# Start bytes of the moving operands: inner activations to byte 192, inputs of the second block and of the last feed-forward to byte 128

## The chip, the core and the metric

The kernel runs on one core of one Trainium2 chip. The metric is the device time of one execution in microseconds; the time before is the median of three runs. The profile is of one further execution, whose own time is given beside its span.

## What is computed

One sequence of 256 tokens with 1024 features, and 256 context tokens, go through two residual blocks of two layers each. All data are float32.

```
first_block, per layer:  h = half_ffn(h); hc = half_ffn(hc)              # SwiGLU, 1024 -> 2 x 2816 -> 1024
                         y, yc = diff_attention (layer 0) | gqa (layer 1)
                         h = gated_residual(h, y); h = half_ffn(h)        # hc too, in layer 0 only
swiglu(h, w_in, w_out):  gate, up = split(h @ w_in); (silu(gate) * up) @ w_out
second_block, per layer: p = rms_norm(x) @ w_in                           # 1024 -> 9180 columns, 18 pieces
                         y_a = sparse attention (8 heads, top 64 keys by an index score)
                         y_b = stick-breaking attention; y_c = chunked mLSTM
                         mixed = sum_g sigmoid(merge_g) * (branch_g @ w_branch_g)
                         x = x + mixed @ w_out
```

## The kernel before

Features lie on the 128 partitions and tokens along the free axis. A weight matrix is loaded by SyncE in pieces of 256 columns (tile `raw`, 1 MB for 1024 rows); ScalarE rounds each half of it to fp32r (`wh`, line 60) and VectorE writes the remainder (`wl`, line 61). The activations are split in the same way, into `xh` and `xl`, `gh` and `gl`, and so on. A product is then three matmuls per 128 rows, in `mm3` (lines 75 to 80): `wh` by the high part (L78), `wh` by the low part (L79), `wl` by the high part (L80), with 128 weight columns stationary and the tokens moving. In the first block 512 tokens move where context and sequence go together (feed-forwards 1 to 3), and 256 in the last feed-forward, which has the sequence alone, in the projections and outputs that are done by halves, and in the whole second block.

The tiles with which this case has to do, by their names in the profile:
- `psg<-xh,wh`: the feed-forward's first product; `psy<-gh,wh`: its second one, from the inner activations `gh`, `gl`. These are written by VectorE at lines 322 and 323, in two tiles per 128 inner features, from the pool `slot` of 16 tiles. The last third of feed-forwards 1 to 3 does half of its output columns by halves, 256 tokens at a time.
- `psy<-oh` and `psy<-ohl`: the attention outputs of the first block, also in `slot`; `adas` (some of the modulation weights) and `tok` (the tokens at the start) are in it too.
- `psp`, `psk`, `psckv<-xh,wh`: the second block's projections, from `xh`, `xl` of the pool `x2`; `psp<-bh,wh`: the branch products, from `bh`, `bl` of the pool `y2`, which holds nearly all other tiles of the second block as well.

A pool's tiles lie one behind another at fixed places, and the pools in the order in which `run` opens them. A moving operand therefore has one start byte per pool, counted here modulo 256. The stationary operands `wh` and `wl` start at byte 192 of 256 everywhere, before and after.

Each engine executes its own instructions in the order in which the code issues them; `wh` and `wl` have four buffers each, `raw` three in the first block and two in the second.

Of the kernel before, what the change touches and what calls it, by code (L numbers as in the profile page):

```python
# [4 lines left out]
F32 = mybir.dt.float32  # L5
F32R = mybir.dt.float32r
# [6 lines left out]
KC = 8  # L13
# [30 lines left out]
class Block:  # L44
# [217 lines left out]
                nc.scalar.activation(self.xh[c][:, s], t, AF.Identity, bias=B)  # L262
                nc.vector.scalar_tensor_tensor(self.xl[c][:, s], t, B, self.xh[c][:, s].bitcast(F32), ALU.add, ALU.subtract)

    def new_x(self, n=512):
        self.xh = [self.xp.tile([128, n], F32R, name=f"xh{c}", tag=f"xh{c}") for c in range(KC)]
        self.xl = [self.xp.tile([128, n], F32R, name=f"xl{c}", tag=f"xl{c}") for c in range(KC)]

    def new_y(self):
        self.y = [self.t2("y") for c in range(KC)]  # L270
# [8 lines left out]
    def ffn(self, i, f, halves, done, fill=(), then=None, mid=None):  # L279
        nc, I = self.nc, self.I  # L280
        w_in, w_out = I['ffn_w_in'][i, f], I['ffn_w_out'][i, f]
        width = 256 * len(halves)
        if len(halves) == 2:
            self.new_y()
        else:
            self.y = self.h[1]

        self.set_fill(fill, DFF // 128 + 4 * (len(PASSES) - 1))
        for pi, (p0, p1) in enumerate(PASSES):
            nk = p1 - p0  # L290
            gh, gl = {}, {}
            for c in range(p0, p1, 2):
                if mid and c == 0:
                    us = mid.pop(0)
                else:
                    us = self.ffn_units(i, f, c)
                tiles = [(w, self.pst("psg")) for w in us]
                if c == 0:
                    for hf, s in [(0, slice(0, width))] if mid else [(hf, HALF[hf]) for hf in halves]:
                        if hf:  # L300
                            self.step_tail(9)

                        order = [(k, u) for k in range(6) for u in tiles] + [(k, u) for u in tiles for k in (6, 7)]
                        for n, (k, (w, ps)) in enumerate(order):
                            if n in (8, 16, 24):
                                self.step_tail()
                            for _ in range((0, 1, 2, 3, 4, 8, 8).count(n) if mid else 0):
                                mid.pop(0)()
                            self.mm3(ps[:, s], w, k, self.xh[k][:, s], self.xl[k][:, s], k == 0, k == 7)
                for j in range(2):  # L310
                    if c > 0:
                        for w, ps in tiles[2 * j:2 * j + 2]:
                            for k in range(KC):
                                self.mm3(ps[:, 0:width], w, k, self.xh[k][:, 0:width], self.xl[k][:, 0:width], k == 0, k == 7)
                    pg, pu = tiles[2 * j][1], tiles[2 * j + 1][1]
                    sg = self.t2("sg")
                    nc.scalar.activation(sg[:, 0:width], pg[:, 0:width], AF.Silu)
                    g = self.t2("g")
                    nc.vector.tensor_mul(g[:, 0:width], sg[:, 0:width], pu[:, 0:width])  # L319
                    a = self.sp.tile([128, 512], F32R, name="gh", tag="slot")  # L320
                    b = self.sp.tile([128, 512], F32R, name="gl", tag="slot")
                    nc.vector.tensor_copy(a[:, 0:width], g[:, 0:width])
                    nc.vector.tensor_sub(b[:, 0:width], g[:, 0:width], a[:, 0:width].bitcast(F32))  # L323
                    gh[c + j], gl[c + j] = a, b
                    self.place()
            last = pi == len(PASSES) - 1
            if last and then:
                self.warm(then)
            self.wout(w_out[p0 * 128:p1 * 128], [gh[k] for k in range(p0, p1)], [gl[k] for k in range(p0, p1)], halves,
                      pi == 0, done if last else None)  # L330
# [1014 lines left out]
    def run(self):  # L1345
        tc, nc, I = self.tc, self.nc, self.I
        from contextlib import ExitStack
        with ExitStack() as es:
            pool = lambda name, bufs, st=es, **kw: st.enter_context(tc.tile_pool(name=name, bufs=bufs, **kw))
            self.during, self.edge, self.ramp = {}, [], []  # L1350
            self.cp = pool("const", 1)
            self.hp = pool("h", 1)
            self.tp = pool("tmp", 2)
            self.wp = pool("w", 4)
            with ExitStack() as e1:
                self.phase = 0
                self.psA = pool("ps", 1, e1, space=PSUM)
                self.xp = pool("x", 1, e1)
                self.yq = pool("yq", 1, e1)
                self.rawp = pool("raw", 3, e1)  # L1360
                self.yp = pool("y", 1, e1)
                self.gp = pool("gt", 3, e1)
                self.sp = pool("slot", 16, e1)
                self.setup()
                self.first_block()
            with ExitStack() as e2:
                self.phase = 1
                self.psA = pool("ps2", 1, e2, space=PSUM)
                self.rawp = pool("raw2", 2, e2)
                self.big = pool("big", 1, e2)  # L1370
                self.small = pool("small", 1, e2)
                self.xp = pool("x2", 1, e2)
                self.yp = pool("y2", 1, e2)
                self.setup2()
                for l in range(2):
                    self.hybrid(l)
                    self.dumph(f's_x_{l}')
                self.final()
# [42 lines left out]
class Join:  # L1421
# [48 lines left out]
    def finish(self, hf):  # L1470

        b, nc = self.b, self.b.nc
        s = HALF[hf]
        A, BC = b.pst("psst")[:, 0:2], b.pst("psst")[:, 0:4]
        for q in range(6):
            dst = A[:, q:q + 1] if q < 2 else BC[:, q - 2:q - 1]
            o = (q // 2 % 2) * 256 + q % 2 * 128
            nc.tensor.matmul(dst, lhsT=self.acc[hf][q // 4][:, o:o + 128], rhs=b.ones[:, 0:1])
        Bs, C = BC[:, 0:2], BC[:, 2:4]
        H = self.H[:, 2 * hf:2 * hf + 2]  # L1480
        r = b.rsqrt(A, 2, 1.0 / D, "r")
        u = b.tiny("u", 2)
        nc.vector.tensor_mul(u, C, r)
        nc.vector.scalar_tensor_tensor(u, Bs, 2.0, u, ALU.mult, ALU.add)
        nc.vector.tensor_mul(u, u, r)
        nc.vector.tensor_add(u, u, H)
        nc.vector.tensor_scalar(u, u, 0.0, None, ALU.max)
        r2 = b.rsqrt(u, 2, 1.0 / D, "p")
        self.rs, self.R, self.ts = (r, r2), None, {}
        if not self.pre:  # L1490
            b.joined = self
            return
        yield
        self.row(0)
        yield
        Rn = self.row(1)
        if not self.ready:
            b.new_x()
            self.ready = True
        for c in range(KC):  # L1500
            self.step(hf, c)
            t = b.tp.tile([128, 256], F32, name="t", tag="t", bufs=4)
            nc.vector.scalar_tensor_tensor(t, b.h[hf][c], self.Gp[:, c, hf:hf + 1], Rn, ALU.mult, ALU.mult)
            B = self.B[:, self.k * 8 + c, hf:hf + 1]
            nc.scalar.activation(b.xh[c][:, s], t, AF.Identity, bias=B)
            b.low(b.xl[c][:, s], t, B, b.xh[c][:, s])
            if c in b.during:
                b.during.pop(c)()
            if hf == 0 and c in (0, 3, 6) and b.ramp:
                b.ramp.pop(0)()  # L1510
# [95 lines left out]
```

## Time and profile before

| | |
|---|---|
| median of 3 runs | 2581.46 us (2580.11 to 2582.78) |
| profiled execution: time, span | 2581.55 us, 2579.8 us |
| TensorE busy | 2475.5 us, 96% of the span |
| VectorE, ScalarE, GpSimd busy | 1429.9, 1036.1, 406.6 us |
| mean granted TensorE clock | 0.983 |
| DMA | 346.56 MB, mean 134 GB/s |

"PE" is TensorE's matmuls and "PEld" its weight loads, which overlap them. The end of a matmul is modelled in the profile and matmuls overlap, so the length of one is not what it costs. What counts is the distance between the starts of two that follow each other, and it is read from the first and the last start of a line's matmuls in a stretch, or from how many fall into it.

### The profile page before, as it was taken

The page shows a single profiled execution, that of the slowest core. Times are in us where ns is not written, and L with a number is a line of the kernel's source. Part 1 is how long each engine was busy: PE and PEld are TensorE (multiplying, and loading weights), DVE is VectorE, ACT ScalarE, POOL GpSimd, SP SyncE. Part 2 cuts the span into 40 slices and gives each one's busy share as a digit, 9 for nine tenths or more (in the row PEclk, how much of TensorE's full clock was granted, in tenths as well). Part 3 has the DMA queues.
Part 4 walks back from the last instruction along what each step waited for, and adds up shares of the span by engine and source line. Part 5 has one row for each costly group of instructions (what it writes and reads, how often), then busy time and mean ns, then how long its engine had stood idle before and what let it go on. Part 6 is the DMA issues. An engine that isn't in the chain of part 4 may idle for free. (4 is left out here: it accounts for less than half of the span.)

```text
span 2579.8 us, 37984 instructions
## 1 busy us (share of the span) xinstructions
PE 2475.5 (96%) x15131; PEld 2091.2 (81%) x15131; DVE 1429.9 (55%) x2478; ACT 1036.1 (40%) x1734; POOL 406.6 (16%) x427
## 2 busy tenths in 40 slices
PE   7999999999999999999999999999979999889998
PEld 3777778666678888878787887789968999879998
DVE  4333337666665333374333377666686765676655
ACT  3222225554453222243222255644545544446443
POOL 1000006221051000061000064310240010201010
PEclk9999998999999999999999999999989999999999
DMA  8453432444532322243422344445633456534454
GB/s 284 145 165 119 159 98 86 128 147 155 160 114 83 114 92 88 98 126 120 147 88 92 98 137 134 142 157 189 200 99 103 128 155 177 156 99 130 139 186 133
DMA packets 321789, 346.56 MB, mean 134 GB/s; under 512 B 23906, under 2 KB 282568, under 8 KB 321612
## 3 DMA queue, kind: packets, MB, share of 16 engines
q1 hardware_dynamic: 320706, 343.35, 42.2%
q8 instruction: 119, 1.95, 0.3%
q10 hardware_dynamic: 906, 0.78, 0.1%
q14 instruction: 58, 0.48, 0.1%
HBM read 343.04 MB, written 1.05 MB: 133 GB/s over the span
## 5 line engine op out<-in xcount | busy, mean ns | idle before, releaser
L60 ACT CAST wh<-raw 128x1024 fp32r<-128x1024 f32 (+2 forms) x534 | 528.2, 998 | 1131.6 <-PE psg L79 554.3
L61 DVE TENSOR_TENSOR wl<-raw,wh 128x1024 fp32r<-128x1024 f32 (+2 forms) x534 | 640.1, 1204 | 562.7 <-ACT wh L60 562.0
L79 PE MATMUL psg<-xl,wh 128*128 128x512 f32 (+1 forms) x1472 | 523.8, 356 | 3.3 <-POOL xl L1286 3.3
L78 PE MATMUL psg<-xh,wh 128*128 128x512 f32 (+1 forms) x1472 | 523.0, 357 | 2.9 <-ACT xh L1313 2.3
L80 PE MATMUL psg<-xh,wl 128*128 128x512 f32 (+1 forms) x1472 | 521.4, 355 | 0.0
L78 PE MATMUL psp<-xh,wh 128*128 128x256 f32 x1248 | 356.6, 286 | 11.9 <-DVE mlu L1147 3.8
L80 PE MATMUL psp<-xh,wl 128*128 128x256 f32 x1248 | 353.9, 284 | 3.2 <-DVE wl L61 3.2
L79 PE MATMUL psp<-xl,wh 128*128 128x256 f32 x1248 | 355.0, 285 | 0.6 <-POOL xl L855 0.6
L78 PEld LDWEIGHTS psg<-xh,wh 128*128 128x128 f32 x1472 | 277.3, 189 | 59.0 <-ACT wh L60 12.6
L79 PEld LDWEIGHTS psg<-xl,wh 128*128 128x128 f32 x1472 | 278.4, 189 | 53.4 <-issue 8.4
L80 PEld LDWEIGHTS psg<-xh,wl 128*128 128x128 f32 x1472 | 278.2, 189 | 39.7 <-issue 0.8
L79 PE MATMUL psy<-gl,wh 128*128 128x512 f32 (+1 forms) x800 | 273.8, 342 | 2.6 <-DVE gl L323 2.5
L78 PE MATMUL psy<-gh,wh 128*128 128x512 f32 (+1 forms) x800 | 275.3, 344 | 0.0
L80 PE MATMUL psy<-gh,wl 128*128 128x512 f32 (+1 forms) x800 | 273.8, 342 | 0.0
L78 PEld LDWEIGHTS psp<-xh,wh 128*128 128x128 f32 x1248 | 236.8, 190 | 20.7 <-issue 5.5
L80 PEld LDWEIGHTS psp<-xh,wl 128*128 128x128 f32 x1248 | 236.9, 190 | 5.0 <-DVE wl L61 4.0
L79 PEld LDWEIGHTS psp<-xl,wh 128*128 128x128 f32 x1248 | 237.3, 190 | 2.8 <-POOL xl L855 1.2
L243 POOL TENSOR_TENSOR acc<-acc,sq 128x256 f32<-128x256 f32 x70 | 57.0, 816 | 1108.2 <-ACT acc L237 1102.5
L319 DVE TENSOR_TENSOR g<-sg,psg 128x512 f32<-128x512 f32 (+1 forms) x88 | 54.6, 620 | 223.4 <-PE psg L80 223.4
L78 PEld LDWEIGHTS psy<-gh,wh 128*128 128x128 f32 x800 | 150.4, 188 | 26.3 <-ACT wh L60 5.0
L79 PEld LDWEIGHTS psy<-gl,wh 128*128 128x128 f32 x800 | 151.1, 189 | 22.9 <-DVE gl L323 3.2
L80 PEld LDWEIGHTS psy<-gh,wl 128*128 128x128 f32 x800 | 150.5, 188 | 21.7 <-issue 1.7
(465 smaller groups left out, 3602.7 us busy)
## 6 DMA issues: line engine op xcount, KB each, us to landing
raw<-in_ffn_w_in SPq DMA_DIRECT2D x88, 1024.0 KB
raw<-in_w_in SPq DMA_DIRECT2D x70, 1024.0 KB
adaw<-in_ada_w SPq DMA_DIRECT2D x240, 256.0 KB
raw<-in_ffn_w_out SPq DMA_DIRECT2D x32, 1024.0 KB
adas<-in_ada_w SPq DMA_DIRECT2D x48, 256.0 KB
raw<-in_ffn_w_out SPq DMA_DIRECT2D x16, 768.0 KB
raw<-in_da_w_in SPq DMA_DIRECT2D x12, 1024.0 KB
raw<-in_w_branch SPq DMA_DIRECT2D x24, 512.0 KB
```

What stands on the lines that cost most here:

```text
L60: a = nc.scalar.copy(wh[:, 0:nk, :], r)
L61: b = nc.vector.tensor_sub(wl[:, 0:nk, :], r, wh[:, 0:nk, :].bitcast(F32))
L78: mm(ps, lhsT=wh[:, k, :], rhs=xh, start=first, stop=False)
L79: mm(ps, lhsT=wh[:, k, :], rhs=xl, start=False, stop=False)
L80: mm(ps, lhsT=wl[:, k, :], rhs=xh, start=False, stop=last)
L243: b = (eng or nc.vector).tensor_tensor(acc, acc, sq, ALU.add)
L319: nc.vector.tensor_mul(g[:, 0:width], sg[:, 0:width], pu[:, 0:width])
```

## The change

Only places in memory change. A 64-byte tile `pad` is put ahead of the pool `slot`, which moves its tiles by 64 bytes, and a 224-byte tile `pad2` ahead of `x2`, which moves the tiles of `x2` and `y2`. In the last feed-forward, where 256 tokens fit into a slot of 512 with room to spare, `gh` and `gl` start 48 elements (192 bytes) into their slot, and its `xh` and `xl` start 48 elements into their tile.

```diff
-    def new_x(self, n=512):
-        self.xh = [self.xp.tile([128, n], F32R, name=f"xh{c}", tag=f"xh{c}") for c in range(KC)]
+    def new_x(self, n=512, at=0):
+        self.xh = [self.xp.tile([128, at + n], F32R, name=f"xh{c}", tag=f"xh{c}")[:, at:at + n] for c in range(KC)]
...
-                    a = self.sp.tile([128, 512], F32R, name="gh", tag="slot")
-                    b = self.sp.tile([128, 512], F32R, name="gl", tag="slot")
+                    at = 0 if width == 512 else 48
+                    a = self.sp.tile([128, 512], F32R, name="gh", tag="slot")[:, at:at + width]
+                    b = self.sp.tile([128, 512], F32R, name="gl", tag="slot")[:, at:at + width]
...
                 self.gp = pool("gt", 3, e1)
+                pool("pad", 1, e1).tile([128, 16], F32, name="pad")
                 self.sp = pool("slot", 16, e1)
...
                 self.small = pool("small", 1, e2)
+                pool("pad2", 1, e2).tile([128, 56], F32, name="pad2")
                 self.xp = pool("x2", 1, e2)
...
         if not self.ready:
-            b.new_x()
+            if len(self.hacc) == 1:
+                b.new_x(256, 48)
+            else:
+                b.new_x()
             self.ready = True
```

What starts where, by the addresses in the two built programs (modulo 512 in brackets, where `wh` and `wl` are at 448). The counts are of matmuls, all three lines together:

| moving operand | tokens | matmuls | byte before | byte after |
|---|---|---|---|---|
| `gh`, `gl`, feed-forwards 1 to 3 | 512 | 1296 | 128 (128) | 192 (192) |
| the same, by halves | 256 | 576 | 128 (128) | 192 (192) |
| `oh`, `ol` (first attention) | 512 | 96 | 128 (128) | 192 (192) |
| the same, by halves | 256 | 192 | 128 (128) | 192 (192) |
| `ohl` (second attention) | 256 | 192 | 128 (128) | 192 (192) |
| `xh`, `xl`, last feed-forward | 256 | 1056 | 192 (448) | 128 (128) |
| `gh`, `gl`, last feed-forward | 256 | 528 | 128 (128) | 128 (384) |
| `xh`, `xl`, second block | 256 | 3888 | 160 (160) | 128 (384) |
| `bh`, `bl`, second block | 256 | 576 | 160 (160) | 128 (384) |
| `xh`, `xl`, feed-forwards 1 to 3 | 512 | 2976 | 192 (448) | 192 (448) |

No instruction is added, removed or moved: apart from line numbers and buffer numbers, the rows of the two programs are the same on each of the five engines, with the same waits. The output is the same computation.

## Rows read from the trace of the kernel before

**Rows 1.** The page: span, and busy time of TensorE.
```profile
span 2579.8 us, 37984 instructions
PE 2475.5 (96%) x15131; PEld 2091.2 (81%) x15131; DVE 1429.9 (55%) x2478; ACT 1036.1 (40%) x1734; POOL 406.6 (16%) x427
```
**Rows 2.** Windows: busy time (instructions) by engine, granted clock, DMA share, GB/s.
```profile
1181.00:1505.00 324.00, 324.00 (x1431) 261.85 (x1428) 123.67 (x151) 86.95 (x118) 20.04 (x21) 1.00 0.33 107
1679.00:1874.00 195.00, 193.15 (x1607) 189.39 (x1604) 125.45 (x187) 91.03 (x134) 28.70 (x28) 0.99 0.58 180
2442.00:2542.00 100.00, 100.00 (x847) 100.00 (x846) 59.32 (x74) 43.25 (x59) 7.22 (x4) 1.00 0.57 180
```
**Rows 3.** Groups by shape, TensorE, one of three lines: count, busy us, mean ns.
```profile
L78 PE MATMUL psp<-xh,wh 128*128 128x256 f32 x1248 | 356.6, 286 | 11.9 <-DVE mlu L1147 3.8 <-ACT xh L854 3.6 <-ACT dq L921 2.3
L78 PE MATMUL psy<-gh,wh 128*128 128x512 f32 x432 | 171.7, 397 | 0.0
L78 PE MATMUL psy<-gh,wh 128*128 128x256 f32 x368 | 103.6, 282 | 0.0
L78 PE MATMUL psp<-bh,wh 128*128 128x256 f32 x192 | 54.1, 282 | 0.0
L78 PE MATMUL psy<-ohl,wh 128*128 128x256 f32 x64 | 18.3, 287 | 0.0
```
**Rows 4.** Line 78 in seven stretches: count, least/median/greatest ns, first and last start.
```profile
L78 PE MATMUL psg<-xh,wh x127: 389/389/395, 1007.1 to 1092.8; 128*128 128x512 f32 x127
L78 PE MATMUL psy<-gh,wh x63: 394/394/394, 962.3 to 1005.7; 128*128 128x512 f32 x63
L78 PE MATMUL psg<-xh,wh x126: 280/283/283, 1738.8 to 1783.8; 128*128 128x256 f32 x126
L78 PE MATMUL psy<-gh,wh x60: 276/276/276, 1784.8 to 1804.9; 128*128 128x256 f32 x60
L78 PE MATMUL psy<-gh,wh x29: 281/281/281, 1864.0 to 1873.9; 128*128 128x256 f32 x29
L78 PE MATMUL psy<-gh,wh x37: 281/281/281, 407.9 to 420.7; 128*128 128x256 f32 x37
L78 PE MATMUL psy<-ohl,wh x56: 276/276/389, 1650.7 to 1669.8; 128*128 128x256 f32 x56
```
**Rows 5.** TensorE in order of time, around 1863 us: start, length, matmul.
```profile
1862.88 0.50 PE L1449 MATMUL psst<-ones,acc 128*128 128x1 f32 x4
1863.24 0.36 PE L78 MATMUL psy<-gh,wh 128*128 128x256 f32 x1
1863.44 0.28 PE L79 MATMUL psy<-gl,wh 128*128 128x256 f32 x1
1863.56 0.28 PE L80 MATMUL psy<-gh,wl 128*128 128x256 f32 x1
```
**Rows 6.** TensorE in order of time, from 1784.0 us.
```profile
1784.02 0.28 PE L80 MATMUL psg<-xh,wl 128*128 128x256 f32 x1
1784.13 0.29 PE L78 MATMUL psy<-gh,wh 128*128 128x256 f32 x1
1784.26 0.28 PE L79 MATMUL psy<-gl,wh 128*128 128x256 f32 x1
```
**Rows 7.** TensorE in order of time, second block, from 1985.8 us.
```profile
1985.83 0.48 PE L1088 MATMUL psz<-sbq,sbk 64*128 64x128 f32 x3
1986.24 0.39 PE L78 MATMUL psp<-xh,wh 128*128 128x256 f32 x1
1986.46 0.28 PE L79 MATMUL psp<-xl,wh 128*128 128x256 f32 x1
```
**Rows 8.** Chain that ended last, shares by line: 1874 to 2226, 2226 to 2569 us.
```profile
by line: issue 19.3%; PE psp L78 12.1%; PE psp L79 12.0%; PE psp L80 11.8%; DMA raw<-in_w_in 7.3%; DVE wl L61 6.2%; ACT wh L60 3.2%; DMA raw<-in_w_out 1.5%; DVE sc L1050 1.4%; DVE m L1049 1.1%; POOL iq L441 1.1%; DVE trot L440 0.9%; POOL sb
by line: issue 42.9%; PE psp L79 8.8%; PE psp L78 8.8%; PE psp L80 8.6%; DVE wl L61 3.7%; DMA raw<-in_w_in 2.3%; ACT wh L60 2.0%; PE psvd L913 1.2%; POOL iq L441 1.1%; DVE trot L440 1.1%; DVE sc L1050 0.9%; POOL sbe L1095 0.9%; DVE mlu L114
```
**Rows 9.** Groups by shape, VectorE: products out of PSUM in the two blocks.
```profile
L319 DVE TENSOR_TENSOR g<-sg,psg 128x512 f32<-128x512 f32 x66 | 45.4, 687 | 208.6 <-PE psg L80 208.6
L1012 DVE SCALAR_TENSOR_TENSOR mg<-mg,psp 128x512 f32<-128x512 f32 x16 | 10.9, 681 | 0.3
```

More of the change, by code (lines that the diff above doesn't have):

```diff
@@ L263, in pre_norm @@
                 nc.vector.scalar_tensor_tensor(self.xl[c][:, s], t, B, self.xh[c][:, s].bitcast(F32), ALU.add, ALU.subtract)
-    def new_x(self, n=512):
-        self.xh = [self.xp.tile([128, n], F32R, name=f"xh{c}", tag=f"xh{c}") for c in range(KC)]
-        self.xl = [self.xp.tile([128, n], F32R, name=f"xl{c}", tag=f"xl{c}") for c in range(KC)]
+    def new_x(self, n=512, at=0):
+        self.xh = [self.xp.tile([128, at + n], F32R, name=f"xh{c}", tag=f"xh{c}")[:, at:at + n] for c in range(KC)]
+        self.xl = [self.xp.tile([128, at + n], F32R, name=f"xl{c}", tag=f"xl{c}")[:, at:at + n] for c in range(KC)]
     def new_y(self):
```

## The prediction

> **What bounds the kernel now.** I read the page first, then windows, then single lines by stretch. The page gives TensorE 2475.5 of 2579.8 us [rows 1]. Windows show that this is no average over idle and busy stages: in feed-forward 3 it is busy for 324.00 of 324.00 us, in the last feed-forward for 193.15 of 195.00, in the dense part of the second block for 100.00 of 100.00, while VectorE, the next engine, has 38, 64 and 59% [rows 2]. The granted clock there is 1.00 or 0.99, the upper of the two levels, so the clock has nothing left to give. A shorter distance between matmuls is therefore a shorter kernel, unless weights come too late.
>
> The change touches nothing but the byte at which moving operands start, so the question is whether matmuls of one shape follow each other at different distances in different places. They do. From first and last start, over the count of all three lines [rows 4]:
> - 512 tokens from byte 192 (`psg`): 85.7 us over 126 x 3 steps, 226.7 ns each; from byte 128 (`psy`): 43.4 over 62 x 3, 233.3 ns.
> - 256 tokens from byte 192 (`psg`): 45.0 over 125 x 3, 120.0 ns; from byte 128 (`psy`): 20.1 over 59 x 3, 113.6 ns in one stretch, and 9.9 over 28 x 3, 117.9 ns in another.
> - 256 tokens from byte 160 (the second block): 847 matmuls in 100 us, and one length of 0.28 us for those that began ahead of the window: 100.28 / 847, 118.4 ns [rows 2].
>
> 226.7 less 120.0 is 106.7 ns for 256 more columns, so at byte 192 a matmul has 13.3 ns beside its columns whatever its width. At byte 128 it is 20 ns at 512 and 7 or 11 at 256. Stationary tiles start at byte 192 in all these rows, the engine waits for nothing in them, and the clock is the same; I find no other difference than the start byte. So the order of merit turns over with the width: 192 is better at 512, 128 at 256. At 128 and 256 tokens there are two rhythms, and rows show how they are entered. After the four one-column matmuls at 1862.88 the first step is 200 ns (1863.24 to 1863.44), and 117.9 follows [rows 4, 5]; the halves at 408 us go at the same slower pace, (420.7 - 407.9) / 108 = 118.5, good to 0.9 ns [rows 4]. Straight out of `psg`, with steps of about 0.12 us at 1784.13, 113.6 follows [rows 4, 6].
>
> **The change, part by part.**
> *Inner activations, 512 tokens, 128 to 192.* 432 x 3 = 1296 matmuls [rows 3] by 233.3 - 226.7 = 6.6 ns: 8.6 us. 96 more of the attention output from the same pool: 0.6. They stand where TensorE never idles [rows 2], so all of it counts: -9.2.
>
> *What rides along in the pool.* 576 half-width matmuls of feed-forwards 1 to 3 (part of the 368 x 3 of [rows 3]) and 192 of the first attention go from 128 to 192, which at 256 tokens is the worse byte: to 120.0 from 117.9, as nearly all start after one-column matmuls like those of [rows 5]. 768 x 2.1 = 1.6 us lost, at most 768 x 6.4 = 4.9 if they were in the quick rhythm. The 192 of `ohl` lose more, 6.4 ns each by 113.6 (their own stretch gives 19.1 / 165 = 115.8 with its interruptions [rows 4]): 1.2. Together +2.8.
>
> *Last feed-forward, 192 to 128.* 1056 matmuls `psg`: 120.0 to 113.6 is 6.8 us, to 117.9 is 2.2. I take the quick rhythm: these stretches begin out of waits or out of each other, and the nearest row, `psy` right behind, took it coming from `psg` [rows 6]. Its `psy` keeps byte 128: 0, bounded below by 441 of the 528 falling to the slower rhythm, +1.9. Weights are no obstacle: TensorE idles 2 of 195 us there, with three `raw` buffers [rows 2]. -6.8.
>
> *Second block, 160 to 128.* 1248 x 3 + 192 x 3 [rows 3] and 144 of the other two projections: 4464 matmuls by 118.4 - 113.6 = 4.8 ns, 21.4 us gross; by 117.9 only 0.5 ns, 2.2 us. Which rhythm? Those that I follow start after a wait with a first step of 220 ns (1986.24 to 1986.46 [rows 7]), not the 200 ns of [rows 5]; the quick rhythm is nearer. But not all of it reaches the end. On the chain, TensorE's projections and "issue" (mostly matmuls that follow each other without a wait) have 19.3 + 35.9 = 55% of the first layer and 42.9 + 26.2 = 69% of the second; the rest is loads of `raw` into two buffers, the split on VectorE and ScalarE, and the index scores [rows 8]. A quicker TensorE waits there for the same weights. 62% of 21.4: -13.3. Bounds: 21.4 and, if weights took everything, 0.
>
> *Everything else that moved.* Some 690 other matmuls of the second block read or write `y2` at a new byte. No row prices them; with the largest step between bytes seen above, 6.6 ns, they are worth at most 690 x 6.6 x 0.62 = 2.8 us either way, and I take 0. VectorE takes 687 ns for a product out of PSUM with tiles at byte 192 and 681 with tiles at byte 160 [rows 9], so for the other engines the byte costs nothing. No wait is added, and no queue is passed.
>
> Sum: -9.2 + 2.8 - 6.8 - 13.3 = -26.5. The profiled execution took 2581.55 us, 0.09 above the median, so **2555.0 us**.
>
> A rule that speaks against this: the Trainium skill, "TensorE: Matmul & The Clock Gate", section "Back-to-back issue gap", gives the distance at full clock as columns / 2.4 + 2.5 ns, thus about 109 and 216 ns, with no place for an address, and its step on loading weights says that the two reading ports of TensorE don't steal from each other. By it the change is worth nothing. The trace disagrees on both: the distances are longer, and differ at equal columns.
>
> **Rivals.**
> *Slower rhythm.* The last feed-forward and the second block settle at 117.9. For it: 117.9 is what most stretches after one-column matmuls have, and the second block is full of such breaks. Against: the 220 ns starts. Time: -9.2 + 2.8 - 2.2 + 1.9 - 1.4 = -8.1, 2573.4. With half of the second block in each rhythm, 7.3 us instead of 13.3: 2561.
>
> *The count is modulo 512, not 256.* The tiles that the change makes are at bytes 192 and 384 of 512; no row has either, rows have 448, 128 and 160. If the period is longer than 256, the 512-token gain may not come (0 instead of -9.2), the halves lose their 2.8, and the last feed-forward's first product, at 128 of 512, gains its 6.8. Were the second block and the last `psy` then at the worst distance that a row has at 256 tokens, 120.0, they would add 4464 x 1.6 x 0.62 = 4.4 and 441 x 6.4 = 2.8: +3.2, 2584.8, slower. Each nanosecond in the second block is worth 4464 x 0.62 = 2.8 us, so without it the sum is -1.2 and it turns at 118.8 ns, 0.4 above today. For it: nothing but the gap in the rows. Against: nothing either, except that 192 and 128 differ, so the period is not 64.
>
> *Weights bind.* The second block gains nothing, as loads and splits set its pace: -13.2, 2568. For it: one load in a chain through two buffers; against it, windows of 100 us without an idle TensorE [rows 2].
>
> *Nothing happens.* The difference between `psg` and `psy` comes from something that I don't see and that stays: 2581.5. The rule quoted above from the Trainium skill ("TensorE: Matmul & The Clock Gate", "Back-to-back issue gap") comes out here too.
>
> **Numbers.** Quick rhythm nearly throughout 0.50; mixed 0.15; slower rhythm 0.16; longer period 0.11; weights bind 0.04; nothing 0.04. The likeliest gives 2555, by itself 2548 to 2562 (from 0.62 to the whole of the second block's gain, and 2.8 for the other matmuls). The first three and weights together are 0.85 and end at 2575 with some us for the halves, so the range is 2548 to 2575. A measurement of this kernel can tell about 0.2% (5 us) from no change. Faster by more: the same four and a part of the longer period, 0.87. Within it: nothing, and part of the longer period, 0.07. Slower: the rest of it, 0.06.
>
> **What the profile after would show.** `psy` at 512 tokens with 226.7 ns between starts, its halves and `ohl` at 120.0; `psg` of the last feed-forward at 113.6; the second block between 113.6 and 117.9, with more idle time of TensorE ahead of `psp` and a larger share of the chain for `raw`, `wh` and `wl`. The prediction is wrong if the second block sits in the slower rhythm, or if 192 or 384 of 512 behave unlike 192 and 128 of 256.

## The result, and the profile after

The changed kernel took 2558.28 us (median of four runs, 2554.82 to 2563.11) against 2581.32 for the kernel before beside it: ratio 0.9912, 95% interval 0.9895 to 0.9929, 23.0 us less. Two more measurements gave 0.9933 (0.9914 to 0.9953) and 0.9918 (0.9902 to 0.9933). The eleven executions that these compare lie from 2554 to 2567 us, median 2562.1. Two further executions of the second measurement took 4017 and 10067 us and are left out of every number here. The prediction was 2555.0, range 2548 to 2575.

The page's first lines of the profiled execution (2557.98 us), which answer [rows 1]:
```profile
span 2556.3 us, 37984 instructions
PE 2447.3 (96%) x15131; PEld 2073.1 (81%) x15131; DVE 1434.3 (56%) x2478; ACT 1035.8 (41%) x1734; POOL 405.9 (16%) x427
```
TensorE is busy for 28.2 us less, and the span is 23.5 us shorter. Line 78 in five stretches of the kernel after, columns as in [rows 4]: 512-token `psy`; its halves; `ohl`; the last feed-forward's `psg`, then its `psy`:
```profile
L78 PE MATMUL psy<-gh,wh x61: 389/389/389, 954.0 to 994.8; 128*128 128x512 f32 x61
L78 PE MATMUL psy<-gh,wh x42: 283/283/368, 403.7 to 419.9; 128*128 128x256 f32 x42
L78 PE MATMUL psy<-ohl,wh x51: 283/283/283, 1639.9 to 1657.9; 128*128 128x256 f32 x51
L78 PE MATMUL psg<-xh,wh x121: 276/276/276, 1723.9 to 1764.7; 128*128 128x256 f32 x121
L78 PE MATMUL psy<-gh,wh x57: 276/276/276, 1769.8 to 1788.8; 128*128 128x256 f32 x57
```
The steps are the first to the last start over three times the count less one: 40.8 / 180 = 226.7 ns, 18.0 / 150 = 120.0 for `ohl`, 40.8 / 360 = 113.3 and 19.0 / 168 = 113.1. The halves show 283 where they had 281. The modelled length follows the distance (283 with 120.0, 281 with 117.8, 275 or 276 with 113.3), so the median length tells at a glance which a stretch has.

The second block did not follow as far. Its projections before and after, then the window that answers to the third of [rows 2], then the chain's two stretches, which answer to [rows 8]:
```profile
L78 PE MATMUL psp<-xh,wh x1248: 274/281/582, 1886.9 to 2569.8; 128*128 128x256 f32 x179
```
```profile
L78 PE MATMUL psp<-xh,wh x1248: 276/276/582, 1869.0 to 2546.3; 128*128 128x256 f32 x179
```
```profile
2420.00:2520.00 100.00, 99.60 (x862) 99.34 (x861) 59.59 (x75) 43.64 (x61) 7.20 (x4) 1.00 0.59 187
```
```profile
by line: issue 20.0%; PE psp L78 13.0%; PE psp L79 12.9%; PE psp L80 12.8%; DVE wl L61 7.1%; DMA raw<-in_w_in 3.9%; ACT wh L60 2.9%; DVE mlu L1148 1.8%; DMA raw<-in_w_out 1.5%; DVE sc L1051 1.4%; POOL iq L442 1.1%; DVE m L1050 1.1%; DVE tro
by line: issue 42.8%; PE psp L79 9.5%; PE psp L78 9.4%; PE psp L80 9.2%; DVE wl L61 4.4%; DVE mlu L1148 1.9%; ACT wh L60 1.7%; POOL iq L442 1.1%; DVE trot L441 1.1%; PE psvd L914 1.0%; DVE sc L1051 0.9%; POOL sbe L1096 0.9%; DVE m L1050 0.8
```
From its first `psp` to the end of the span it took 692.9 us before (2579.8 - 1886.9) and 687.3 after. The window holds 862 matmuls instead of 847, 1.8% more, where 113.6 ns for 118.4 would make 4% more. All steps without a stop (distances under 135 ns) have a mean of 118.3 before and 115.4 after: 56% are quick (about 113.3 ns), and most of the others are in the slower rhythm of 117.8.

By stretches, from the first matmul of each to that of the next (us, after minus before):

| stretch | predicted | this execution |
|---|---|---|
| feed-forwards 1 to 3 and both attention outputs (A, B) | -6.4 | -3.1 - 1.3 - 4.2 + 0.2 = -8.4 |
| last feed-forward (C) | -6.8 | -5.0 |
| second block (D) | -13.3 | -5.6 |
| start and both attentions | 0 | -0.4 - 2.2 - 1.9 = -4.5 |
| sum | -26.5 | -23.5 |

So the sum came out near, but not term by term: the second block brought less than half of its forecast, and the attentions, forecast at nothing, made up for a part of that.

### The profile page after: what moved, and what is told of

Same layout as the page of the kernel before. It is cut to its first block, busy times and chain, and to the rows that moved or that the text cites. A ratio compares the mean times of both kernels' runs of the same rounds, so it can differ in the third digit from the quotient of the medians.

```text
span 2556.3 us, 37984 instructions
## 1 busy us (share of the span) xinstructions
PE 2447.3 (96%) x15131; PEld 2073.1 (81%) x15131; DVE 1434.3 (56%) x2478; ACT 1035.8 (41%) x1734; POOL 405.9 (16%) x427
## 5 line engine op out<-in xcount | busy, mean ns | idle before, releaser
L78 PEld LDWEIGHTS psy<-gh,wh 128*128 128x128 f32 x800 | 151.2, 189 | 23.5 <-ACT wh L60 5.0
L80 PEld LDWEIGHTS psy<-gh,wl 128*128 128x128 f32 x800 | 151.2, 189 | 18.7 <-issue 1.7
```

The source lines that it names most:

```text
L78: mm(ps, lhsT=wh[:, k, :], rhs=xh, start=first, stop=False)
L80: mm(ps, lhsT=wl[:, k, :], rhs=xh, start=False, stop=last)
```

## Experiments

**The parts by themselves.** Theory: each group of matmuls has its distance by its byte, and the parts add up. Rivals: the joints hide parts of them, or the second block's loads bind.

```diff
# slot_only: the kernel before with
+                    at = 0 if width == 512 else 48
...
+                pool("pad", 1, e1).tile([128, 16], F32, name="pad")
```


> The inner activations and attention outputs alone at byte 192 (feed-forwards 1 to 3, both attentions); last feed-forward's first product and second block as before. By the prediction's sum (A -9.2, B +2.8): -6.4 us. If the halves' loss is hidden behind the joining work at the ends of the feed-forwards: -8.5 to -9.2. If the marks of the two profiled executions are taken at their word, where the attentions gained 4 us although none of their own operands moved: about -13. In all three the 512-token psy should stand at 226.7 ns, halves at 120.0. (The inner activations of the last feed-forward stay at byte 128, at 384 of 512 as in the change.)

Measured: 0.9958 (0.9944 to 0.9972), -10.8 us, range -14.5 to -7.2. Matmul by matmul against the kernel before, steady distances alone: 512-token `psy` -8.2 us and attention outputs -0.3 (predicted -8.6 and -0.6); halves of feed-forwards +1.4 and of the first attention +0.5 (predicted together +1.6); `ohl` +1.1 (+1.2). A and B are thus sized rightly as work, but for the attention outputs at 512 tokens (half of what was forecast). The stops of `psst` and `psada` beside `ohl` got 1.3 us shorter, so that its 1.1 cost nothing. The two attentions, whose operands keep their offsets, got 1.8 and 1.6 us shorter; the granted clock was higher there, which has a paragraph at the end.

```diff
# second_only: the kernel before with
+                pool("pad2", 1, e2).tile([128, 56], F32, name="pad2")
```


> The inputs of the second block alone at byte 128. By the prediction: -13.3 us, nearly all matmuls in the quick rhythm at 113.6 ns. By what the changed kernel's execution shows (56 per cent of the steady steps quick, mean 115.4, and part of that waited away in front of loads): -5 to -6. If the slower rhythm held nearly throughout: -0.3 to -1.4.

Measured: 0.9976 (0.9966 to 0.9987), -6.2 us. The second block took 683.9 us, with 72% of its steps quick, mean 114.7. The mixed account holds (-5 to -6 expected), the quick one (-13.3) falls.

```diff
# lastff_only: the kernel before with
-            b.new_x()
+            if len(self.hacc) == 1:
+                b.new_x(256, 48)
...
+                pool("pad2", 1, e2).tile([128, 56], F32, name="pad2")
```


> The inputs xh, xl of the last feed-forward alone at byte 128. By the prediction: 1056 x 6.4 = -6.8 us, psg at 113.6 ns. If the time is partly taken by waits at the stage's ends, as the marks of the two profiled executions have it: -5.0. If psg took the slower rhythm without the other edits: -2.2, at 117.9 ns.

As the diff shows, this kernel held `pad2` as well, so it is the last feed-forward and the second block together, not the first alone as the expectation has it. Measured: 0.9955 (0.9941 to 0.9970), -11.6 us; less the -6.2 of the second block alone, some -5 for the last feed-forward. Its `psg` stood at 113.4, the stretch took 195.0 us instead of 201.4.

> The whole change again, beside its three parts on the same chip. If the parts add up, its gain is the sum of theirs; from the first measurement -23.0 us. If the parts hide each other's gains at the joints, it is less than their sum. With two rhythms that are chosen anew at each stop, its runs should lie further apart (8.3 us in the first measurement) than those of the kernel before (2.7).

Measured: 0.9933 from two executions, -17.3 us (-22 to -12). The parts make -10.8 - 11.6 = -22.4, just beyond that interval, and near the -23.0 and -21.0 of the other two measurements: they add up as far as this can tell. The profile gave one thing more. Line 78 in the last feed-forward, where the first execution had 276:
```profile
L78 PE MATMUL psg<-xh,wh x180: 276/281/281, 1690.0 to 1769.7; 128*128 128x256 f32 x180
```
The same program, in another execution, has 26% of these steps quick, most of the others at 117.8, and a mean of 116.7; the stretch took 201.0 us. So the byte alone does not give the quick rhythm, on which C was built.

**What the byte is counted from.** The table ahead of the prediction counts bytes from the memory's start; the weights stood at 192 in all of it.

```diff
# weights_moved: the changed kernel with
+            pool("padw", 1).tile([128, 16], F32, name="padw")
             self.wp = pool("w", 4)
+            pool("padv", 1).tile([128, 48], F32, name="padv")
```


> The changed kernel with all weights wh, wl at byte 0 of 256 instead of 192; every moving operand stays where the change put it. If the moving operand's own byte decides: 226.7 ns at 512 and 120.0 at 256 for byte 192, 113.3 or 117.8 for byte 128, and a time of 2555 to 2564 us like the changed kernel's. If the offset between the two decides: moving minus weights, now 0 at most places, becomes 192, and -64 becomes 128; then distances at 512 tokens move off 226.7, by the one other row up to 233.3, which over 2976 + 1296 + 96 matmuls at 512 tokens would be up to 29 us more.

Measured: 2598.91 us in one execution, 40 more than the change. Line 78, `psg` at 512 tokens, whose byte is still 192:
```profile
L78 PE MATMUL psg<-xh,wh x110: 394/394/394, 1018.6 to 1094.9; 128*128 128x512 f32 x110
```
76.3 / 327 = 233.3 ns, where it had 226.7 in [rows 4]. The second block, now 128 bytes behind the weights, went to 118.8. The moving operand's own byte falls as the cause, since it did not move; what is left is its offset behind the weights, or the byte of the weights. The next kernel tells these apart.

The kernel `micro` leaves out the whole computation: it has nothing but such matmuls, in groups of 24, with no load and no other engine beside them, at 16 start bytes of the moving operand (`xo`, in elements of 4 bytes) and four of the weights (`wo`). Its core is
```python
for wo in (0, 16, 32, 48):
    for n in (512, 256):
        for xo in range(0, 64, 4):
            self.group(n, xo, wo)
```


> Leaves out the whole computation: only matmuls of the same form, in the same triples of wh by high, wh by low, wl by high part, 24 to a group, with nothing beside them on other engines or queues; start bytes of the moving operand in steps of 16, of the weights in steps of 64, 512 and 256 columns, then 256 columns after one-column matmuls and after waits of many lengths. Theory 1, the start byte alone decides, counted from the memory: with weights at byte 192 the kernel's numbers return, 226.7 ns at byte 192 and 233.3 at 128 for 512 columns; 120.0 at 192, 118.4 at 160, 113.3 or 117.8 at 128 for 256; and the weights' byte changes nothing. Theory 2, the offset between moving operand and weights decides: the same table, but moved along by 64 with each 64 bytes that the weights move. Rival, the other traffic of the kernel (loads, VectorE, ScalarE) decides and the byte only goes along with it: one distance, 216 to 227 ns and 109 to 120 ns, at all bytes. If the rhythm at byte 128 is chosen at each stop, entries of different lengths there give both 113.3 and 117.8; at byte 192 all give 120.0.

The order of time on TensorE, weights at byte 192: a group's first matmul at offset 96, at offset 112, and the first of the next group:
```profile
320.53 0.28 PE L16 MATMUL pb<-XH,WH 128*128 128x256 f32 x1
...
323.41 0.28 PE L16 MATMUL pa<-XH,WH 128*128 128x256 f32 x1
...
326.13 0.28 PE L16 MATMUL pb<-XH,WH 128*128 128x256 f32 x1
```
2.88 / 24 = 120.0 ns at offset 96 and 2.72 / 24 = 113.3 at 112. With the weights at byte 0, again a group at offset 112, 2.72 us:
```profile
469.17 0.28 PE L16 MATMUL pa<-XH,WH 128*128 128x256 f32 x1
...
471.89 0.39 PE L16 MATMUL pb<-XH,WH 128*128 128x512 f32 x1
```
Mean distance in a group by offset modulo 256 (ns, the usual value of the four places of the weights; in 28 of the 32 cases all four agree within 0.7):

| offset | 0 | 16 | 32 | 48 | 64 | 80 | 96 | 112 |
|---|---|---|---|---|---|---|---|---|
| 512 columns | 228.3 | 231.4 | 233.5 | 233.1 | 229.3 | 230.8 | 233.8 | 231.2 |
| 256 columns | 119.6 | 119.0 | 116.9 | 118.3 | 117.8 | 119.8 | 120.0 | 113.3 |

| offset | 128 | 144 | 160 | 176 | 192 | 208 | 224 | 240 |
|---|---|---|---|---|---|---|---|---|
| 512 columns | 232.7 | 233.3 | 233.8 | 233.2 | 233.0 | 234.4 | 232.9 | 227.0 |
| 256 columns | 118.3 | 118.7 | 117.3 | 119.2 | 113.8, once 117.7 | 119.3 | 118.3 | 117.3 |

(The first steps of a group are in the mean; at offset 0 the later ones stand at 226.7 and 120.0.) Theory 2 holds, theory 1 and the rival of other traffic fall: at one offset, four bytes of the weights give one distance. Why the offset matters, no run shows. The kernel before had offset 0 (inputs of the feed-forwards), 192 (inner activations) and 224 (second block), and the table gives back its distances: 226.7, 233.3 [rows 4] and 118.4 [rows 2].

The rhythm at offset 192. After three one-column matmuls (six records, of which the last five stand in one row) and after four:
```profile
618.01 0.70 PE L16 MATMUL pt<-A 128*128 128x1 f32 x5
618.57 0.36 PE L16 MATMUL pb<-XH,WH 128*128 128x256 f32 x1
618.77 0.28 PE L16 MATMUL pb<-XL,WH 128*128 128x256 f32 x1
...
619.70 0.28 PE L16 MATMUL pb<-XH,WH 128*128 128x256 f32 x1
...
624.00 0.28 PE L16 MATMUL pb<-XH,WL 128*128 128x256 f32 x1
624.12 0.94 PE L16 MATMUL pt<-A 128*128 128x1 f32 x8
624.93 0.36 PE L16 MATMUL pa<-XH,WH 128*128 128x256 f32 x1
625.13 0.28 PE L16 MATMUL pa<-XL,WH 128*128 128x256 f32 x1
...
626.07 0.28 PE L16 MATMUL pa<-XH,WH 128*128 128x256 f32 x1
...
630.54 0.28 PE L16 MATMUL pa<-XH,WL 128*128 128x256 f32 x1
```
From the tenth to the last of the 48 it is 4.30 / 38 = 113.2 ns in the first case and 4.47 / 38 = 117.6 in the second, after the same first step of 0.20 us. After 1, 3, 5 and 7 one-column matmuls it was 113.3, after 2, 4, 6 and 8 117.8, and after 16 waits of many lengths 113.3 each time. At offset 0, 64 and 224 the same entries gave one rhythm (119.8 to 120.0, 117.8, 118.2 to 118.4). So at offset 192 what comes ahead of a stretch picks the rhythm, and it is held until the next stop. The parity is no rule, though: after 11 it was 117.8 (after 9, 10 and 12 the granted clock fell within the stretch), and in these entries the output tile, `pa` or `pb`, alternates along with the count. The waits had 113.3 with either tile.

**Does an offset with one rhythm do better?** `offset_112` puts the 256-token operands of the last feed-forward and the second block's `xh`, `xl` there, and leaves `bh`, `bl` at offset 192 by other pads (not shown here):
```diff
-                    at = 0 if width == 512 else 48
+                    at = 0 if width == 512 else 28
-                b.new_x(256, 48)
+                b.new_x(256, 28)
-        self.new_x(256)
+        self.new_x(256, 4, 320)      # second block: tiles of 320, used from element 4
```


> The changed kernel, with the moving operands of 256 tokens of the last feed-forward (both products) and the xh, xl of the second block 112 bytes behind the weights (byte 48 of 256) instead of 192; in the measured groups of 24 all four places at that offset gave 113.3 ns, where 192 gave 113.8 or 117.7. Theory, the offset decides and the rhythm falls away: 113.3 ns in nearly all steady steps of these groups; last feed-forward 195 us in every execution (201.0 in one with the slower rhythm); second block, with a mean of 114.8 ns so far and 7.0 of 15.7 us gained there, another 0.45 x 3888 x 1.5 = 2.6 us; in all 2552 to 2556 us, and runs closer together than the 8.3 us of the change. Rival, the kernel's interruptions bring a second rhythm here too, or the gain is waited away: 2558 to 2564 us, as the change itself.

Measured: 2560.27, 0.9916 (0.9904 to 0.9929): no better than the change. The distances came as the theory has it, 97% of the last feed-forward's steps quick, 82% of those of `xh`, `xl` in the second block; the second block took 683.9 us (2553.7 - 1869.8):
```profile
span 2553.7 us, 37984 instructions
L78 PE MATMUL psp<-xh,wh x1248: 275/275/582, 1869.8 to 2543.7; 128*128 128x256 f32 x179
```
The rival's second half holds for the time of the whole. In this one execution the second block was 2.3 us below the mean of five executions at offset 192 (686.2), and as short as the shortest of them.

**What takes the second block's gain.** First the other way:

```diff
# second_offset_96: the kernel before with
+                pool("pad2", 1, e2).tile([128, 96], F32, name="pad2")
```


> The kernel before, with the inputs of the second block 96 bytes behind the weights, the worst offset of the measured groups at 256 columns (120.0 ns). Theory: steps of 120.0 instead of 118.3, thus 4464 x 1.7 = 7.6 us gross. If the second block passes on the share that it passed on at offset 192 (7.0 of 15.7 us, 45 per cent): +3.4 us. If a loss counts in full, since a slower TensorE gets its weights in time anyway: +7.6. If the pace of loads and splits rules: 0.

Measured: 1.0019 (1.0010 to 1.0029), +4.9 us, between the first two expectations. Steps stood at 119.9, thus (119.9 - 118.3) x 4464 = 7.1 us gross, and the second block took 698.8 us, 6 more:
```profile
span 2584.4 us, 37984 instructions
L78 PE MATMUL psp<-xh,wh x1248: 274/282/579, 1885.6 to 2574.4; 128*128 128x256 f32 x179
```
A loss is passed on at 5 to 6 of 7 us, a gain at about half. Something stands close behind TensorE. The next pair loads only half of the rows of the second block's weights (`wh` and `wl` are made from that half twice), once with the bytes of before and once with `xh`, `xl` at offset 112 and `bh`, `bl` at 192:
```diff
-        self.nc.sync.dma_start(raw[:, 0:nk, 0:cols], src.rearrange("(k p) c -> p k c", p=128))
+        src = src.rearrange("(k p) c -> p k c", p=128)
+        n = nk // 2 if self.phase else nk
+        self.nc.sync.dma_start(raw[:, 0:n, 0:cols], src[:, 0:n, :])
```


> The kernel before with half of the bytes of most weight loads of the second block: only the first half of the rows of a raw tile is loaded, and both halves of wh and wl are made from it (the result is another one). If loads are what the second block waits for, it is shorter than the 692 to 693 us of the kernel before by more than 10 us; if it waits for the split on VectorE and ScalarE and for the branches' own chains, by less than 5. It stands beside the run at offset 112 with the same loads.

> The same with half of the loads of the second block, and its xh, xl 112 bytes behind the weights, bh and bl 192 bytes: (118.3 - 113.3) x 3888 + 576 x 3.5 = 21.5 us gross against the run before. If it was the loads that took the second block's gain, nearly all of it arrives: 15 to 21 us less than with the same loads at the old byte. If the gain is lost to the split and the branches' chains, the share stays near 45 per cent: 9 to 11 us.

Measured: 2575.44 (0.9976) and 2563.83 (0.9934). Spans and first `psp` of the one and the other (line 83 here is line 78 of the other kernels):
```profile
span 2572.8 us, 37977 instructions
L83 PE MATMUL psp<-xh,wh x1248: 276/281/582, 1885.1 to 2562.5; 128*128 128x256 f32 x179
```
```profile
span 2560.6 us, 37977 instructions
L83 PE MATMUL psp<-xh,wh x1248: 275/275/583, 1885.1 to 2550.3; 128*128 128x256 f32 x179
```
687.7 and 675.5 us. Half of the loads are worth 5 us at the old offset, between the two bounds expected (more than 10, less than 5). At the quick one 12.2 us of 17 gross arrive ((118.3 - 114.4) x 4464), 70%; with all loads it was 692.9 - 683.9 = 9.0 of 17, about half. Neither expectation is met whole (15 to 21, or 9 to 11): loads take part of the gain. That the split and the branches' own chains take the rest is not shown.

Is it the loads' rate, or the two buffers? `raw_3` is the change with a third:
```diff
-             {"d": 10, "e": 7, "m": 7, "t": 1, "th": 2, ...
+             {"d": 9, "e": 7, "m": 6, "t": 1, "th": 2, ...
-                self.rawp = pool("raw2", 2, e2)
+                self.rawp = pool("raw2", 3, e2)
```


> The changed kernel with a third raw buffer in the second block; its place comes from one buffer each of the tile groups d and m (9 and 6 instead of 10 and 7). Halving the loads took 5.2 us off the second block at the old byte and 12.2 us more at offset 112, so loads hold back a quick TensorE. If that is because a load can't begin before one of two buffers is free: second block 675 to 682 us instead of 683.9 to 687.3, the whole 4 to 10 us less than the change beside it. If it is the rate at which the loads come, a third buffer changes nothing: within 2 us of the change. If the two missing buffers of d and m cost more than the loads: 2 us or more above it.

> The change itself, beside the run with three raw buffers and with as many rounds as the run at offset 112. By its first measurement 2558.3 us, ratio 0.9912. If the two rhythms at offset 192 make the spread of its runs, their mix in the second block and the last feed-forward differs from execution to execution, and its times run over some 8 us, 2555 to 2564; but the runs at offset 112, where the last feed-forward has one rhythm alone, were 8.3 us apart too, which speaks for the granted clock (0.981 to 0.985 there) as the source.

Measured: 2546.61 us, 0.9865 (0.9850 to 0.9880), beside 2562.11 of the change on the same chip: 15.5 us less than the change and some 35 less than the kernel before. Span, first `psp` and the chain in the second block's first layer:
```profile
span 2538.4 us, 37980 instructions
L78 PE MATMUL psp<-xh,wh x1248: 275/276/682, 1870.1 to 2528.5; 128*128 128x256 f32 x179
by line: issue 19.5%; PE psp L79 15.2%; PE psp L78 15.1%; PE psp L80 15.0%; DVE wl L61 6.9%; DVE mlu L1148 2.5%; DVE sc L1051 1.4%; DVE m L1050 1.2%; DVE trot L441 1.2%; POOL iq L442 1.1%; ACT wh L60 1.1%; POOL sbe L1096 0.9%; DVE trot L440
```
The second block took 668.3 us, below what was expected. The loads are gone from the chain's larger shares, where the change had 3.9 + 1.5%, and TensorE's own went from 39 to 45%. So the rate of the loads did not bind; with more places to load into, the same loads came in time. Part of it is the rhythm: 84% of the steps were quick here, with a mean of 114.1 ns where five executions with two buffers had 115.0, which is 4.0 us over 4464 steps. What the third buffer is worth with the old bytes was not measured. The second block got 24.6 us shorter than before, and its steps account for (118.3 - 114.1) x 4464 = 18.7 of that, so at least some 6 us are the buffer's own; how the rest divides stays open.

## Why the prediction was right, and which terms were not

**A, B.** Right as work, and as mechanism with one correction: what counts is the offset behind the weights, and as these stood still, the byte told the same. -8.5 and +3.0 were measured, -9.2 and +2.8 forecast. Part of B was hidden by stops that got shorter.

**C, last feed-forward.** Where the rhythm was the quick one, the work was right: (119.9 - 113.6) x 1056 = 6.7 us, 6.8 forecast. The stretch got 5.0 us shorter in the profiled execution, at a mean granted clock of 0.97, and 5.9 and 6.4 in two others, at 0.98 as before. But "I take the quick rhythm" was luck. In four executions at that byte the stretch took 195.0 to 196.6 us, in a fifth, with the slower rhythm, 201.0; forecast 194.6. The rule by which it was chosen, a first step of 200 or 220 ns, does not hold: both rhythms begin with a first step of 0.20 us in the rows of `micro` above. In the second blocks of the six executions at that byte, `raw_3` included, 121 of 202 stretches (of eight steps and more) with a first step of 190 to 212 ns went on quickly, and 143 of 185 with one of 212 to 240: a first step near 220 makes the quick rhythm likelier, no more. The same rule stood behind D. The window of [rows 2], besides, is not the stage: the last feed-forward runs from 1685.5 to 1886.9 us, and TensorE is busy there for 192.4 of 201.5.

**D, second block: mis-sized by more than half.** Forecast 113.6 ns and a share of 62% from the chain's rows; measured in five executions 114.5 to 115.7 ns, mean 115.0, and 683.9 to 688.7 us, mean 686.2: (692.9 - 686.2) / ((118.3 - 115.0) x 4464) = 45%, and 4.2 to 9.0 us instead of 13.3. The step that failed is the term's size, in both factors: steps that were all taken as quick, and a share read from a chain of the kernel before, as if each stretch of TensorE's on it could shrink freely. Behind it stood, in part, loads into two buffers, as the third buffer shows; [rows 2], with a TensorE that never idles for 100 us, hid that. The sign that was forecast, a larger share of the chain for `raw`, `wh` and `wl`, came for `wl` alone (6.2 to 7.1% in the first layer); `raw<-in_w_in` fell from 7.3 to 3.9%, so the chain's shares did not show it either. The rival "weights bind" had the right place and got 4 in 100; what happened lies between it and the mixed case.

**Everything else, 0.** The attentions brought -4.1 us in the profiled execution, at a higher granted clock (below). No term forecast it, and for the first attention it was luck. It made up for nearly half of what C and D lacked, so the profiled sum came out nearer than its terms; the median of all runs, 2562, is 7 us above the forecast and inside its range.

**The rival of a period longer than 256** fell: 192 and 384 of 512 behave like 448 and 128. The period is in the offset, which no row of the kernel before could show, as the weights stood still.

## What to carry to other kernels

Where such matmuls follow each other without a wait, the place of the moving operand relative to the stationary one is worth up to 3% at 512 columns and 6% at 256 (here 226.7 to 234.4, 113.3 to 120.0): move both together and the distances stay, move the weights alone and they change. Before an engine's speed-up is costed by its share of the chain, ask how late the next supplier is; a run with the engine made slower, and one with the loads halved, tell it. A third buffer (15.5 us beside the change) was worth more here than an offset with one rhythm (nothing in the time of the whole).

## What was not expected of the hardware

The offset itself, modulo 256 and in steps as small as 16 bytes, in a kernel without any other traffic. The Trainium skill, "TensorE: Matmul & The Clock Gate", section "Back-to-back issue gap", has for matmuls by themselves one distance for a width, whatever the address (the prediction quoted the formula without that limit). The nearest that a run came to its 109 and 216 ns is 113.3 and 226.7.

The clock of the attentions. Windows at the same place of the program, kernel before, kernel after (the granted clock is third from the end):
```profile
440.00:470.00 30.00, 26.61 (x153) 24.99 (x153) 18.16 (x44) 13.95 (x29) 13.67 (x16) 0.73 0.17 54
1586.00:1594.00 8.00, 7.21 (x37) 6.13 (x36) 3.94 (x11) 1.80 (x3) 2.09 (x2) 0.79 0.40 131
```
```profile
436.40:466.40 30.00, 26.51 (x168) 23.96 (x167) 21.45 (x52) 16.19 (x31) 15.38 (x18) 0.87 0.22 67
1574.90:1582.90 8.00, 7.19 (x44) 6.03 (x44) 5.47 (x15) 2.57 (x4) 2.72 (x4) 1.00 0.40 131
```
Both stretches have stops of TensorE for the joining work; in the second, some starts of 512 columns are 0.43 us apart in the kernel before, 0.23 after. The lower of the two levels is 1.2 GHz, and the part of an attention that is spent there differs from one execution to another. The first attention took 256.7 to 257.2 us, at a mean granted clock of 0.97, in six executions, and 259.0 to 259.2, at 0.95, in six others. That does not go with the bytes: `second_only`, which leaves the first block as it was, is among the shorter, and `after_again`, the whole change, among the longer. The second attention took 105.4 to 105.7 us, at 0.98, in five of the six executions with `slot` moved, and 107.0 to 108.2, at 0.95 to 0.98, in the sixth and in all six with `slot` at its old byte; whether the change does this by moving the times of the stops is not shown.

The runs of the change with a granted clock of 0.986 lie at 2554 and 2555 us and the one with 0.980 at 2567, which speaks for the clock, and not the rhythm alone, as the source of their spread; `offset_112`, nearly without the second rhythm, spreads as far (8.3 us). What sets that the clock falls in one execution and not in the other stays open.
